# Attention emitted in steps, operands one piece at a time, reciprocals as powers on GpSimd

## Chip, cores and metric

One Trainium2 chip, one core. The metric is the device time of one execution in microseconds, the median of several runs. Engines are called PE (TensorE), DVE (VectorE), ACT (ScalarE), POOL (GpSimd) and SP (SyncE, which issues most DMAs here); PEld is PE's weight load.

## What is computed

Two transformer-like blocks run one after the other over 1024 tokens of width 1024 in fp32. The second one has, between two gated feed-forward layers, a mixer whose first half is attention: eight heads of width 64, three dilated causal windows merged by their softmax denominators. The reference, cut to the attention:

```python
DILATED_BRANCHES = ((128, 1), (512, 4), (2048, 16))

def dilated_window_branch(q, k, v, slopes, window, dilation):
    ...
    s = jnp.einsum('brnqhe,brnkhe->brnhqk', qb, kk) * (HEAD_DIM ** -0.5)
    ...
    s = jnp.where(valid[None, None, :, None], s + bias, -jnp.inf)
    m = jnp.max(s, axis=-1, keepdims=True)
    p = jnp.exp(s - m)
    denom = jnp.sum(p, axis=-1, keepdims=True)
    o = jnp.einsum('brnhqk,brnkhe->brnqhe', p, vv)
    o = o * jnp.swapaxes(1.0 / denom[..., 0], -1, -2)[..., None]
    ...

def second_block(x, ...):
    ...
        q, k, v, u = jnp.split(proj, [ATTN_WIDTH, 2 * ATTN_WIDTH, 3 * ATTN_WIDTH], axis=-1)
        attn = dilated_attention(q, k, v).astype(x.dtype)
        ssm = s5_mixer(u, ...).astype(x.dtype)
        mixed = jnp.concatenate([attn, ssm], axis=-1) @ w_mix_out[l]
    ...
```

The three windows together are one causal softmax over all 1024 keys with a bias that holds slope, mask and the logarithm of how many windows contain a key; the kernel computes it so.

## The kernel before

The whole program is one long sequence of stages; fp32 products are made from pairs of shortened operands, a high part (hi, wh, ph) and what is left (lo, wl, pl), each product being two or three matmuls. A high part is a copy on ACT into a rounded type, a low part a subtraction on POOL or DVE.

The attention stands in the second mixer (mixer2), after the glu of its other half and ahead of the output projection (down, L455). The glu ends in sigmoids on ACT (L1520) and products on DVE (L1521). The stages around it load weights: raw by DMA on SP, wh on ACT (L351), wl on POOL (L352).

Work is done in 16 units, a unit being one half (512 queries) of one of eight heads. For a head, heads_in makes three operands: qq (the query's high half from ACT in 64 partitions, its low part from POOL, L1568, in the other 64), kd (the key's high part, copied by ACT and by a DMA into the other 64 partitions) and kl (the key's low part, POOL L1569, and its DMA). head_v makes vv, the values' two parts. Then softmax does, for each of the unit's four blocks c of 128 queries, with width w = 128 to 512 in the first half and 640 to 1024 in the second:

- logits on PE: kd (L1601) and kl (L1602) against qq into one PSUM bank;
- DVE adds the bias and finds the minimum of the negated logits (L1604) into P;
- ACT takes the exponential in place and its sum into den (L1607);
- DVE makes the reciprocal of den, one column (L1608);
- POOL scales P by it (L1609).

values, for each of 4 or 8 key tiles kt: PE transposes the blocks of P (L1624), ACT copies them as ph (L1626), DVE makes pl (L1627), PE multiplies both by vv into po (L1628, L1629). At the end ACT and DVE add the halves of po into at (L1631, L1632). After all units hilo makes hi (ACT, L1501) and lo (POOL, L1504) of the four at.

The attention loop calls softmax for a unit and then values for the unit three before, each as a whole; heads_in makes two heads at a time and one pair ahead. What an engine then executes is a fixed queue in order: a scheduler, when the program is built, orders each queue by what is emitted and by its own timing estimates, so neighbouring units mix to some degree. Buffers: 32 tiles of 128x1024 shared by operands and probabilities, 8 PSUM banks, two tiles for bias and other large loads (tag xr).

Of the kernel before, what the change touches and what calls it, by code (L numbers as in the profile page):

```python
# [11 lines left out]
F32 = mybir.dt.float32  # L12
F32R = mybir.dt.float32r
# [5 lines left out]
P = 128  # L19
# [228 lines left out]
class Model:  # L248
# [1308 lines left out]
    def heads_in(self, q, k):  # L1557
# [3 lines left out]
        res = []  # L1561
        for a in range(2):
            me, other = slice(64 * a, 64 * a + 64), slice(64 - 64 * a, 128 - 64 * a)
            qq, kd, kl = self.u("qq", F32R), self.u("kd", F32R), self.u("kl", F32R)
            nc.scalar.activation(qq[me], q[me], AF.Copy)
            nc.scalar.activation(kd[me], k[me], AF.Copy)
            nc.sync.dma_start(out=kd.bitcast(F32)[other], in_=kd.bitcast(F32)[me])
            nc.gpsimd.tensor_tensor(qq[other], q[me], qq.bitcast(F32)[me], op=ALU.subtract)  # L1568
            nc.gpsimd.tensor_tensor(kl[me], k[me], kd.bitcast(F32)[me], op=ALU.subtract)  # L1569
            nc.sync.dma_start(out=kl.bitcast(F32)[other], in_=kl.bitcast(F32)[me])  # L1570
            res.append((qq, kd, kl))
        return res
# [9 lines left out]
    def softmax(self, ops, bias, half):  # L1582
# [3 lines left out]
        if half:  # L1586
            ps = [self.u("P") for _ in range(4)]
        else:
            two = [self.u("P", shape=[P, 2, H]) for _ in range(2)]
            ps = [two[c // 2][:, c % 2] for c in range(4)]  # L1590
        mx, den = self.sm("mx", 8), self.sm("den", 4)
        for c, p in enumerate(ps):
# [15 lines left out]
            nc.vector.reciprocal(den[:, c : c + 1], den[:, c : c + 1])  # L1608
            nc.gpsimd.tensor_scalar(out=p[:, :w], in0=p[:, :w], scalar1=den[:, c : c + 1], scalar2=None, op0=ALU.mult)  # L1609
        return ps  # L1610

    def values(self, vv, a, ps, half, at):
# [6 lines left out]
        for kt in range(last + 1):  # L1619
# [9 lines left out]
            nc.tensor.matmul(po[:, sl], vv[:, kt, :], pl[:, sl], start=False, stop=kt == last)  # L1629
        t = self.tmp("vo")  # L1630
        nc.scalar.activation(t[me], po[other], AF.Copy)  # L1631
        nc.vector.tensor_tensor(at[me, half * H : half * H + H], po[me], t[me], op=ALU.add)  # L1632

    def attention(self, qk):

        at, late = [], []
        ops = [self.heads_in(*qk[0])]
        for j in range(4):
            at.append(self.u("at"))
            for a in range(2):  # L1640
                h = 2 * j + a
                bias = self.raw(self.a["bias"][h], name="bias", tag="xr")
                if a == 0 and j < 3:
                    ops.append(self.heads_in(*qk[j + 1]))
                vv = self.head_v(h)
                for half in range(2):
                    ps = self.softmax(ops[j][a], bias, half)
                    late.append((vv, a, ps, half, at[j]))
                    if len(late) > 3:
                        self.values(*late.pop(0))  # L1650
        while late:
            self.values(*late.pop(0))
        return [self.hilo(t) for t in at]
# [71 lines left out]
```

## Time and profile before

| | us |
|---|---|
| median of 3 runs (3076.66 to 3080.45) | 3077.05 |
| the profiled execution | 3082.47 |
| its span | 3080.7 |
| PE busy | 2821.6 (92%) |
| DVE busy | 1775.9 (58%) |
| ACT busy | 1323.5 (43%) |
| POOL busy | 868.0 (28%) |

All trace times are counted from the start of that span. The page cuts the span into 40 slices of 77.0 us and gives each engine's busy share in tenths; the groups of instructions give busy time, mean duration and the idle time ahead of them; the waits say who waited for whom. A share over the whole span says little of one stage, so the rows below are mostly of the attention, 2089.5 to 2271 us.

### The profile page before, as it was taken

Reading aid. Unit: us, or ns where it says so; the run is one execution under the profiler, and the core shown is the slowest. Engines: PE = TensorE matmul, PEld = TensorE weight load, DVE = VectorE, ACT = ScalarE, POOL = GpSimd, SP = SyncE. Lnnn points to the kernel's source line nnn. Section 1 sums busy time; section 2 is a strip of 40 time slices with the busy share of each in tenths; the row PEclk is TensorE's granted clock in tenths of the full one; section 3 lists DMA queues with packets and bytes.
Section 4 is the critical chain, followed back from the end, with each engine's and each line's share of the span. In section 5 each row is a group of like instructions: output and inputs, shape, how many; then the busy total and the mean of one; then the engine's idle time right before and its main releaser. Section 6 shows DMA issues by size and latency. Waiting matters only on the chain.

```text
span 3080.7 us, 33834 instructions
## 1 busy us (share of the span) xinstructions
PE 2821.6 (92%) x12585; PEld 2306.2 (75%) x12585; DVE 1775.9 (58%) x2527; ACT 1323.5 (43%) x1921; POOL 868.0 (28%) x667
## 2 busy tenths in 40 slices
PE   8998999898999979999978999997689899998998
PEld 7777788677777858777767778886677677776776
DVE  4576655487784365665667551417635756665445
ACT  5446555433445463333324452246644533333343
POOL 3331332211222432121111031459844212211002
PEclk9999999999999989999989999998899999999999
DMA  3114344564455123454466661523113244446556
GB/s 141 61 42 137 132 146 146 201 230 144 162 183 170 55 82 103 151 177 150 146 221 212 217 220 72 168 76 110 35 48 130 86 150 158 158 157 208 181 180 209
DMA packets 192309, 443.11 MB, mean 144 GB/s; under 512 B 23220, under 2 KB 23312, under 8 KB 192144
## 3 DMA queue, kind: packets, MB, share of 16 engines
q1 hardware_dynamic: 155600, 362.83, 35.4%
q10 hardware_dynamic: 36544, 78.13, 7.2%
q8 instruction: 98, 1.61, 0.2%
q14 instruction: 67, 0.55, 0.1%
HBM read 303.92 MB, written 131.60 MB: 141 GB/s over the span
## 4 chain that ended last, share of the span: by engine, by line
PE 62%; DMA 14%; DVE 9%; ACT 6%; issue 6%; POOL 2%; SPq 1%; ACTq 0%; DVEq 0%; POOLq 0%
PE b L541 22%; PE b L717 17%; PE b L455 4%; PE b L442 4%; DMA raw<-in_f_out 3%; DMA raw<-in_f_in 3%; DMA td<-tw 2%; DMA tw<-raw 2%; PE b L1103 2%; PE b L1101 2%; PE b L1102 2%; DMA sd<-hs 1%; ACT wh L481 1%; PE b L1624 1%; DVE wl L482 1%
## 5 line engine op out<-in xcount | busy, mean ns | idle before, releaser
L541 PE MATMUL b<-zh,wh 128*128 128x512 f32 x1680 | 644.9, 397 | 30.5 <-ACT wh L481 23.1
L541 PE MATMUL b<-zh,wl 128*128 128x512 f32 x1680 | 623.3, 392 | 8.4 <-DVE wl L482 3.3
L541 PE MATMUL b<-zl,wh 128*128 128x512 f32 x1560 | 612.8, 393 | 15.4 <-DVE zl L211 15.4
L717 PE MATMUL b<-tt,wh 128*128 128x512 f32 x1232 | 392.1, 400 | 51.8 <-ACT tt L698 46.5
L541 PEld LDWEIGHTS b<-zh,wh 128*128 128x128 f32 x1680 | 319.5, 190 | 117.2 <-ACT wh L481 35.1
L541 PEld LDWEIGHTS b<-zh,wl 128*128 128x128 f32 x1680 | 316.8, 189 | 78.6 <-DVE wl L482 4.6
L717 PE MATMUL b<-wl,wh 128*128 128x512 f32 x1344 | 323.5, 402 | 40.3 <-ACT wl L698 26.3
L541 PEld LDWEIGHTS b<-zl,wh 128*128 128x128 f32 x1560 | 295.4, 189 | 79.5 <-DVE zl L211 19.2
L717 PEld LDWEIGHTS b<-wl,wh 128*128 128x128 f32 x1344 | 258.7, 194 | 102.4 <-ACT wl L698 27.8
L717 PEld LDWEIGHTS b<-tt,wh 128*128 128x128 f32 x1232 | 237.5, 194 | 106.8 <-ACT tt L698 48.9
L482 POOL TENSOR_TENSOR wl<-raw,wh 128x1024 fp32r<-128x1024 f32 x60 | 148.0, 2469 | 392.4 <-ACT wh L481 368.9
L698 ACT ACTIVATE wh<-sd 128x1024 fp32r<-128x1024 f32 x140 | 141.7, 1014 | 254.3 <-PE b L717 127.0
L717 PE MATMUL b<-tt,wl 128*128 128x512 f32 x616 | 244.1, 397 | 0.0
L352 POOL TENSOR_TENSOR wl<-raw,wh 128x1024 fp32r<-128x1024 f32 (+1 forms) x58 | 142.6, 2464 | 305.0 <-ACT wh L351 274.1
L481 ACT ACTIVATE wh<-raw 128x1024 fp32r<-128x1024 f32 x120 | 126.8, 1059 | 226.0 <-DMA raw<-in_f_in 102.6
L383 POOL TENSOR_SCALAR v<-ss 128x1 f32<-128x1 f32 x80 | 46.4, 580 | 497.6 <-ACT junk L376 493.9
L618 POOL TENSOR_TENSOR hw<-h 128x512 f32<-128x512 f32 x38 | 59.2, 1558 | 409.2 <-DVE h L1188 173.2
L699 DVE TENSOR_TENSOR tt<-td,tt 128x1024 fp32r<-128x1024 f32 x84 | 95.2, 1134 | 115.4 <-ACT tt L698 115.2
L698 ACT ACTIVATE tt<-td 128x1024 fp32r<-128x1024 f32 x84 | 83.0, 988 | 162.7 <-DMA td<-tw 86.2
L699 DVE TENSOR_TENSOR wl<-sd,wh 128x1024 fp32r<-128x1024 f32 x84 | 97.4, 1159 | 77.1 <-ACT wh L698 77.1
L505 DVE TENSOR_TENSOR s<-raw 128x512 f32<-128x512 f32 x60 | 75.2, 1253 | 115.2 <-DMA raw<-in_f_in 105.2
L717 PEld LDWEIGHTS b<-tt,wl 128*128 128x128 f32 x616 | 119.1, 193 | 25.3
(362 smaller groups left out, 5301.0 us busy)
## 6 DMA issues: line engine op xcount, KB each, us to landing
sd<-hs SPq DMA_DIRECT2D x126, 512.0 KB, 4.0
raw<-in_f_in SPq DMA_DIRECT2D x94, 512.0 KB, 3.5
raw<-in_f_out SPq DMA_DIRECT2D x44, 512.0 KB, 3.6
tw<-raw SPq DMA_DIRECT2D x44, 512.0 KB, 2.9
wd<-in_w_down ACTq DMA_DIRECT2D x40, 512.0 KB, 8.9
td<-tw ACTq DMA_DIRECT2D x40, 512.0 KB, 4.3
hs<-h SPq DMA_DIRECT2D x38, 512.0 KB, 3.3
hs<-hw SPq DMA_DIRECT2D x38, 512.0 KB, 3.1
```

Of the source, the lines that this page charges most:

```text
L352: nc.gpsimd.tensor_tensor(l, r, h.bitcast(F32), op=ALU.subtract)
L442: nc.tensor.matmul(pp[n], w[:, k, :], z(m, k, slice(n * H, n * H + H)), start=k == 0 and w is wh and m == 0, stop=k == nk - 1 and w is wl)
L455: yield nc.tensor.matmul(pp, h[:, ts], w[:, sl], start=f == 0 and w is wh and h is hh, stop=f == len(hs) - 1 and h is hl)
L481: nc.scalar.activation(hi.rearrange("p a b -> p (a b)"), x, AF.Copy)
L482: eng.tensor_tensor(lo.rearrange("p a b -> p (a b)"), x, hi.bitcast(F32).rearrange("p a b -> p (a b)"), op=ALU.subtract)
L505: v.tensor_tensor(s1, a21, a22, op=ALU.add)
L541: self.mark = nc.tensor.matmul(bank, w, x, start=start and k == 0 and i == 0, stop=k == 3 and i == 2, skip_group_check=True)
L698: nc.scalar.activation(hi[:, :n], x[:, :n], AF.Copy)
L699: v.tensor_tensor(lo[:, :n], x[:, :n], hi.bitcast(F32)[:, :n], op=ALU.subtract)
L717: self.mark = nc.tensor.matmul(bank, x[:, c, ts], y[:, c], start=start and k == 0, stop=stop and k == 2, skip_group_check=True)
L1101: nc.tensor.matmul(pp, zh, wh[:, k % 2, :], start=k == 0, stop=False)
L1102: nc.tensor.matmul(pp, zh, wl[:, k % 2, :], start=False, stop=False)
```

## The change

The units and their arithmetic stay, apart from the reciprocal. softmax and values become generators that stop after a query block and after a key tile. attention steps them in turn: for step n, values of unit n-3 (LAG = 3) by key tiles, and between them the query blocks of unit n, so that four blocks are spread over four or eight key tiles. heads_in becomes head_in, which returns two pieces for one head, left (qq) and right (kd, kl); with head_v as third piece, they are emitted one at a time in the second and fourth block of a step, for the next head only. The bias of the next head is requested at the start of a head. The four DVE reciprocals of a unit become one power of -1 on POOL over all four columns of den (128x4, against a tile mone of -1), and the four scalings on POOL follow it.

```diff
-    def heads_in(self, q, k):
...
+    def head_in(self, q, k, a, res):
...
+        def left():
+            qq = self.u("qq", F32R)
             nc.scalar.activation(qq[me], q[me], AF.Copy)
+            nc.gpsimd.tensor_tensor(qq[other], q[me], qq.bitcast(F32)[me], op=ALU.subtract)
+            res.append(qq)
+
+        def right():
+            kd, kl = self.u("kd", F32R), self.u("kl", F32R)
             nc.scalar.activation(kd[me], k[me], AF.Copy)
             nc.sync.dma_start(out=kd.bitcast(F32)[other], in_=kd.bitcast(F32)[me])
-            nc.gpsimd.tensor_tensor(qq[other], q[me], qq.bitcast(F32)[me], op=ALU.subtract)
             nc.gpsimd.tensor_tensor(kl[me], k[me], kd.bitcast(F32)[me], op=ALU.subtract)
             nc.sync.dma_start(out=kl.bitcast(F32)[other], in_=kl.bitcast(F32)[me])
-            res.append((qq, kd, kl))
-        return res
+            res.extend((kd, kl))
+
+        return [left, right]
...
-            nc.vector.reciprocal(den[:, c : c + 1], den[:, c : c + 1])
+            yield
+        nc.gpsimd.tensor_tensor(den, den, self.mone, op=ALU.pow)
+        for c, p in enumerate(ps):
+            w = (4 * half + c + 1) * P
             nc.gpsimd.tensor_scalar(out=p[:, :w], in0=p[:, :w], scalar1=den[:, c : c + 1], scalar2=None, op0=ALU.mult)
-        return ps
...
             nc.tensor.matmul(po[:, sl], vv[:, kt, :], pl[:, sl], start=False, stop=kt == last)
+            if kt < last:
+                yield
...
+    LAG = 3
...
-                if a == 0 and j < 3:
-                    ops.append(self.heads_in(*qk[j + 1]))
-                vv = self.head_v(h)
-                for half in range(2):
-                    ps = self.softmax(ops[j][a], bias, half)
-                    late.append((vv, a, ps, half, at[j]))
-                    if len(late) > 3:
-                        self.values(*late.pop(0))
...
+        def prepare(h):
+
+            ops, vv = [], []
+            bias = self.raw(self.a["bias"][h], name="bias", tag="xr")
+            heads[h] = ops, bias, vv
+            return [*self.head_in(*qk[h // 2], h % 2, ops), lambda: vv.append(self.head_v(h))]
+
+        for f in prepare(0):
+            f()
+        for n in range(16 + self.LAG):
+            h, half = divmod(n, 2)
+            soft = None
+            if h < 8:
...
+                    todo = prepare(h + 1) if h < 7 else []
+                ops, bias, vv = heads[h]
+                ps = []
+                soft = self.softmax(ops, bias, half, ps)
+                late.append((vv[0], h % 2, ps, half, at[h // 2]))
+            val, nk = None, 4
+            if n >= self.LAG:
+                job = late.pop(0)
+                val, nk = self.values(*job), 4 + 4 * job[3]
+            for k in range(nk):
+                if val:
+                    next(val, None)
+                if soft and k * 4 % nk == 0:
+                    next(soft)
+                    if k * 4 // nk in (1, 3) and todo and (half or k * 4 // nk == 1 or len(todo) > 2):
+                        todo.pop(0)()
+            if soft:
+                next(soft, None)
```

The queues of the built program, at three places. POOL around the operands of a head, before: numbers behind a name tell buffers apart, P and den are a unit's probabilities and sums, four query blocks of 128 to 512 being the first half of a head and 640 to 1024 the second.

```order
L1568 TENSOR_TENSOR qq_15533<-qk_14977,qq_15533 64x1024
L1569 TENSOR_TENSOR kl_15535<-qk_14980,kd_15534 64x1024
L1568 TENSOR_TENSOR qq_15542<-qk_14977,qq_15542 64x1024
L1569 TENSOR_TENSOR kl_15544<-qk_14980,kd_15543 64x1024
L1609 TENSOR_SCALAR P_15554<-P_15554,den_15557 128x128
L1609 TENSOR_SCALAR P_15554<-P_15554,den_15557 128x256
L1609 TENSOR_SCALAR P_15555<-P_15555,den_15557 128x384
L1609 TENSOR_SCALAR P_15555<-P_15555,den_15557 128x512
L1609 TENSOR_SCALAR P_15672<-P_15672,den_15677 128x640
L1609 TENSOR_SCALAR P_15673<-P_15673,den_15677 128x768
L1609 TENSOR_SCALAR P_15674<-P_15674,den_15677 128x896
L1609 TENSOR_SCALAR P_15675<-P_15675,den_15677 128x1024
```

The same place in the changed program, operands of one head and one pair of units:

```order
L1566 TENSOR_TENSOR qq_15785<-qk_14977,qq_15785 64x1024
L1615 TENSOR_TENSOR den_15752<-den_15752,mone_15277 128x4
L1573 TENSOR_TENSOR kl_15902<-qk_14980,kd_15901 64x1024
L1615 TENSOR_TENSOR den_15872<-den_15872,mone_15277 128x4
L1618 TENSOR_SCALAR P_15749<-P_15749,den_15752 128x128
L1618 TENSOR_SCALAR P_15749<-P_15749,den_15752 128x256
L1618 TENSOR_SCALAR P_15750<-P_15750,den_15752 128x384
L1618 TENSOR_SCALAR P_15750<-P_15750,den_15752 128x512
L1618 TENSOR_SCALAR P_15867<-P_15867,den_15872 128x640
L1618 TENSOR_SCALAR P_15868<-P_15868,den_15872 128x768
L1618 TENSOR_SCALAR P_15869<-P_15869,den_15872 128x896
L1618 TENSOR_SCALAR P_15870<-P_15870,den_15872 128x1024
```

Before, the operands of two heads come in a row and then scalings alone. Now one head's qq and kl stand between the powers, the power of the second half stands ahead of the first half's scalings, and all eight scalings follow in a row.

POOL at the end of the attention, where lo are the low halves of the finished at; the last of the scalings before:

```order
L1609 TENSOR_SCALAR P_16650<-P_16650,den_16652 128x384
L1609 TENSOR_SCALAR P_16650<-P_16650,den_16652 128x512
L1609 TENSOR_SCALAR P_16767<-P_16767,den_16772 128x640
L1609 TENSOR_SCALAR P_16768<-P_16768,den_16772 128x768
L1609 TENSOR_SCALAR P_16769<-P_16769,den_16772 128x896
L1609 TENSOR_SCALAR P_16770<-P_16770,den_16772 128x1024
L1504 TENSOR_TENSOR lo_17074<-at_15295,hi_17073 128x1024
L1504 TENSOR_TENSOR lo_17078<-at_15530,hi_17077 128x1024
L1504 TENSOR_TENSOR lo_17082<-at_15979,hi_17081 128x1024
```

and now:

```order
L1615 TENSOR_TENSOR den_16624<-den_16624,mone_15277 128x4
L1504 TENSOR_TENSOR lo_17028<-at_15293,hi_17027 128x1024
L1504 TENSOR_TENSOR lo_17032<-at_15516,hi_17031 128x1024
L1615 TENSOR_TENSOR den_16741<-den_16741,mone_15277 128x4
L1504 TENSOR_TENSOR lo_17036<-at_15953,hi_17035 128x1024
L1618 TENSOR_SCALAR P_16621<-P_16621,den_16624 128x128
L1618 TENSOR_SCALAR P_16621<-P_16621,den_16624 128x256
L1618 TENSOR_SCALAR P_16622<-P_16622,den_16624 128x384
L1618 TENSOR_SCALAR P_16622<-P_16622,den_16624 128x512
L1618 TENSOR_SCALAR P_16736<-P_16736,den_16741 128x640
L1618 TENSOR_SCALAR P_16737<-P_16737,den_16741 128x768
L1618 TENSOR_SCALAR P_16738<-P_16738,den_16741 128x896
```

Three of the four low halves moved from behind the last eight scalings to ahead of them, next to the last power.

PE where the logits of a head's first half begin, with P the transposes of an earlier unit; before:

```order
L1601 MATMUL b_15773<-kd_15308,qq_15307 128x128
L1602 MATMUL b_15773<-kl_15309,qq_15307 128x128
L1601 MATMUL b_15780<-kd_15308,qq_15307 128x256
L1602 MATMUL b_15780<-kl_15309,qq_15307 128x256
L1601 MATMUL b_15787<-kd_15308,qq_15307 128x384
L1602 MATMUL b_15787<-kl_15309,qq_15307 128x384
L1629 MATMUL po_15722<-pl_15729,vv_15403 128x512
L1601 MATMUL b_15794<-kd_15308,qq_15307 128x512
L1602 MATMUL b_15794<-kl_15309,qq_15307 128x512
```

The same in the changed program, from the third of the head's kd matmuls (the first two, with eight transposes behind each, stand just ahead of this piece):

```order
L1607 MATMUL b_15810<-kd_15683,qq_15567 128x384
L1636 MATMUL po_15737<-ph_15763,vv_15376 128x512
L1637 MATMUL po_15737<-pl_15764,vv_15376 128x512
L1632 MATMUL b_15815<-idn_78,P_15431 128x128
L1632 MATMUL b_15815<-idn_78,P_15432 128x128
L1632 MATMUL b_15815<-idn_78,P_15433 128x128
L1636 MATMUL po_15737<-ph_15774,vv_15376 128x512
L1637 MATMUL po_15737<-pl_15775,vv_15376 128x512
L1632 MATMUL b_15825<-idn_78,P_15432 128x128
L1632 MATMUL b_15825<-idn_78,P_15433 128x128
L1636 MATMUL po_15737<-ph_15793,vv_15376 128x512
L1608 MATMUL b_15753<-kl_15684,qq_15567 128x128
```

Before, each kd matmul has its kl matmul directly behind it. Now the kd matmuls of three blocks and 21 transposes of the other unit come first and the kl matmuls after them. On SP the order was bias, kd, kd, bias, kl, kl for a pair of heads and is now kd, bias, kl for one head.

## Rows read from the trace of the kernel before

**Rows 1.** page, busy tenths of PE and POOL in 40 slices of the span

```profile
PE   8998999898999979999978999997689899998998
...
POOL 3331332211222432121111031459844212211002
```

**Rows 2.** end of the attention: PE's timeline, then the chain of work

```profile
2259.55 0.30 PE L1624 MATMUL b<-idn,P 128*128 128x128 f32 x1
...
2271.08 19.13 PE b L455 x76
```

**Rows 3.** busy time of each engine by stage; columns in the first line

```profile
core 0: us, PE busy (x) PEld busy (x) DVE busy (x) ACT busy (x) POOL busy (x), PEclk, DMA share, GB/s
2089.50:2271.00 181.50, 130.33 (x674) 109.04 (x673) 125.51 (x378) 125.12 (x267) 145.46 (x80) 0.87 0.18 55
...
2105.90:2205.60 99.70, 69.50 (x358) 60.02 (x358) 66.81 (x212) 68.47 (x148) 98.80 (x54) 0.83 0.20 55
2205.60:2248.60 43.00, 31.45 (x173) 27.05 (x172) 31.12 (x96) 29.45 (x66) 27.35 (x17) 0.90 0.08 26
```

**Rows 4.** waits in the attention: engine, line, releaser, us, times, longest

```profile
PE po L1628 <- ACT ph L1626: 36.7, 17, 7.8
...
POOL P L1609 <- DVE den L1608: 15.6, 5, 6.2
...
PE b L1624 <- POOL P L1609: 6.5, 3, 3.7
```

**Rows 5.** timeline of POOL: start, us, instructions [idle before, releaser]

```profile
2100.66 2.92 POOL L1609 TENSOR_SCALAR P<-P,den 128x128 f32<-128x128 f32 x3
...
2240.99 7.61 POOL L1609 TENSOR_SCALAR P<-P,den 128x768 f32<-128x768 f32 x3 [0.15 <-DVE den L1608]
2248.56 7.07 POOL L1504 TENSOR_TENSOR lo<-at,hi 128x1024 fp32r<-128x1024 f32 x3
```

**Rows 6.** groups of POOL in the attention: busy us, mean ns, idle before

```profile
L1609 POOL TENSOR_SCALAR P<-P,den 128x640 f32<-128x640 f32 (+5 forms) x64 | 109.6, 1734 | 15.9 <-DVE den L1608 15.6
L1568 POOL TENSOR_TENSOR qq<-qk,qq 64x1024 fp32r<-64x1024 f32 x4 | 9.9, 2480 | 0.3
...
L1569 POOL TENSOR_TENSOR kl<-qk,kd 64x1024 fp32r<-64x1024 f32 x4 | 9.5, 2383 | 0.3
```

**Rows 7.** DMA issues: KB each, median us to landing

```profile
kl<-kl SPq DMA_DIRECT2D x8, 256.0 KB, 3.8
```

**Rows 8.** small operations: by line (min/median/max ns), then groups

```profile
L383 POOL TENSOR_SCALAR v<-ss x80: 190/248/1287, 6.2 to 3071.4; 128x1 f32<-128x1 f32 x80
...
L384 POOL TENSOR_TENSOR r<-v,mh x80: 547/548/1617, 6.5 to 3072.2; 128x1 f32<-128x1 f32 x80
...
L1379 POOL TENSOR_TENSOR ph<-s5p,s5k 128x4 f32<-128x4 f32 x8 | 2.0, 253 | 24.2 <-DVE h L1183 20.6 <-DVE sxb L1325 3.6
...
L1608 DVE RECIPROCAL den<-den 128x1 f32<-128x1 f32 x64 | 9.2, 154 | 8.1 <-ACT P L1607 7.9
```

**Rows 9.** timeline of PE and ACT around the first exponentials

```profile
2089.32 0.62 PE L442 MATMUL b<-hi,wl 128*128 128x512 f32 x2
...
2091.22 1.06 ACT L351 ACTIVATE wh<-raw 128x1024 fp32r<-128x1024 f32 x1 [5.65 <-DMA raw<-in_w_mo]
2092.19 1.25 ACT L1520 ACTIVATE gs<-b,cv 128x512 f32<-128x512 f32 x2
...
2093.45 1.28 ACT L1607 ACT_TABLE_LOAD   x1
2094.75 0.40 ACT L1607 ACTIVATE P<-P,mx 128x128 f32<-128x128 f32 x1
...
2098.72 0.71 ACT L1607 ACTIVATE P<-P,mx 128x512 f32<-128x512 f32 x1
...
2115.45 1.04 ACT L1565 ACTIVATE qq<-qk 64x1024 fp32r<-64x1024 f32 x1
```

**Rows 10.** waits of the later stages

```profile
PE b L717 <- ACT tt L698: 10.2, 2, 5.1
```

More of the change, by code (lines that the diff above doesn't have):

```diff
@@ L1555, in v_proj @@
                     self.nc.scalar.activation(o, i, AF.Copy)
[L1557 removed]
+    def head_in(self, q, k, a, res):
         nc = self.nc
[L1561 to L1564, printed above, removed]
+        me, other = slice(64 * a, 64 * a + 64), slice(64 - 64 * a, 128 - 64 * a)
+        def left():
+            qq = self.u("qq", F32R)
             nc.scalar.activation(qq[me], q[me], AF.Copy)
+            nc.gpsimd.tensor_tensor(qq[other], q[me], qq.bitcast(F32)[me], op=ALU.subtract)
+            res.append(qq)
+        def right():
+            kd, kl = self.u("kd", F32R), self.u("kl", F32R)
             nc.scalar.activation(kd[me], k[me], AF.Copy)
             nc.sync.dma_start(out=kd.bitcast(F32)[other], in_=kd.bitcast(F32)[me])
[L1568 removed]
             nc.gpsimd.tensor_tensor(kl[me], k[me], kd.bitcast(F32)[me], op=ALU.subtract)
             nc.sync.dma_start(out=kl.bitcast(F32)[other], in_=kl.bitcast(F32)[me])
[L1571 to L1572 removed]
+            res.extend((kd, kl))
+        return [left, right]
     def head_v(self, h):
@@ L1580, in head_v, with softmax @@
         return vv
-    def softmax(self, ops, bias, half):
+    def softmax(self, ops, bias, half, ps):
         nc = self.nc
@@ L1586, in softmax @@
         if half:
-            ps = [self.u("P") for _ in range(4)]
+            ps.extend(self.u("P") for _ in range(4))
         else:
             two = [self.u("P", shape=[P, 2, H]) for _ in range(2)]
-            ps = [two[c // 2][:, c % 2] for c in range(4)]
+            ps.extend(two[c // 2][:, c % 2] for c in range(4))
         mx, den = self.sm("mx", 8), self.sm("den", 4)
@@ L1632, in values @@
         nc.vector.tensor_tensor(at[me, half * H : half * H + H], po[me], t[me], op=ALU.add)
+    LAG = 3
     def attention(self, qk):
[L1636 to L1642, printed above, removed]
-                if a == 0 and j < 3:
-                    ops.append(self.heads_in(*qk[j + 1]))
-                vv = self.head_v(h)
-                for half in range(2):
-                    ps = self.softmax(ops[j][a], bias, half)
-                    late.append((vv, a, ps, half, at[j]))
-                    if len(late) > 3:
-                        self.values(*late.pop(0))
-        while late:
-            self.values(*late.pop(0))
+        nc = self.nc
+        self.mone = self.sm("mone", 4)
+        nc.vector.memset(self.mone, -1.0)
+        at, late, heads = [], [], {}
+        def prepare(h):
[9 more added lines that the diff above has]
+            if h < 8:
+                if half == 0:
+                    if h % 2 == 0:
+                        at.append(self.u("at"))
+                    todo = prepare(h + 1) if h < 7 else []
[16 more added lines that the diff above has]
+                next(soft, None)
         return [self.hilo(t) for t in at]
```

## The prediction

> **What bounds the kernel now.** I began with the page. PE falls to 7, 6 and 8 tenths in three slices near 2080 to 2310 us, and exactly there POOL, elsewhere mostly at 1 to 4 tenths, reaches 9, 8 and 4 [rows 1]. That is the attention, the only place where the change acts: the first logits follow the glu at 2089.5, and the output projection (L455) starts at 2271.08 [rows 2], 181.5 us in all. The table of stages splits it: over the whole stretch PE is busy 130.3, DVE 125.5, ACT 125.1 and POOL 145.5 us, so POOL is fullest; from 2105.9 to 2205.6 POOL is busy 98.8 of 99.7 us, with PE at 69.5, DVE at 66.8 and ACT at 68.5 [rows 3]. In those 100 us POOL is the bound. Afterwards it is not: of the 43 us from 2205.6 on, it is busy 27.4 [rows 3], and it waits 15.6 us for reciprocals that DVE has not reached [rows 4].
>
> The waits mislead here. The largest by far is PE's for ACT's copy of the transposed probabilities, 36.7 us; PE's direct wait for POOL's scaling is only 6.5 us [rows 4]. But those transposes read probabilities that POOL scaled, and every engine works in order, so a POOL that is behind also holds the logits queued behind the transposes. An edit that removes the 36.7 us by finer interleaving gains only as far as POOL lets it.
>
> POOL's queue: the scaling (L1609) starts at 2100.66, its last three instructions run from 2240.99 to 2248.60, and three low halves of the output (lo, L1504) come after it [rows 5]. From the last scaling to L455 pass another 22.5 us, in which the values of the last units run.
>
> **The change part by part.**
>
> *Values by key tiles between logits.* It adds no arithmetic; it removes phases in which ACT does only exponentials or only copies. As long as POOL is the bound this is worth nothing in the middle. It is worth something at two places, both inside the sum below: POOL's idle 15.9 us (scaling row, [rows 6]) goes, and at the end the values of fewer units are still open.
>
> *Operands one head at a time.* Before, the operands of heads 0 to 3 (eight POOL instructions qq, kl) were made under the glu, where POOL cost nothing, and eight more inside the attention [rows 6]. Now only head 0 and the qq of head 1 come before the first power; kl of head 1 and both of heads 2 to 7, 13 instructions, stand in the POOL-bound queue. At (2.48+2.38)/2 = 2.43 us [rows 6] that is 31.6 us where it was 19.4. DMAs: kd and kl of a head leave SP singly, and the load of the next-but-one bias now stands between them; kl takes 3.8 us to land [rows 7]. On ACT the copies are only spread.
>
> *Reciprocals.* 64 DVE instructions of 154 ns go [rows 8]; DVE is not the bound and the 9.2 us are hidden by POOL, so I count nought. Sixteen POOL powers of 128x4 come, none of which the trace shows. The nearest rows [rows 8]: the same power on 128x1 takes 547 ns in its undisturbed cases, a 128x1 tensor_scalar 190 ns at least, a 128x4 product 253 ns. So one column's power costs about 547-190 = 357 ns over the frame. If one pass serves all four columns, a power is 253+357 = 0.61 us; if columns follow each other, 253+4x357 = 1.68 us. Outer bounds are 0.55 (four columns no dearer than one) and 4x547 = 2.19 us. The rows do not decide between one pass and four; I take the middle, 1.15 us: 16x1.15 = 18.4 us, all on POOL.
>
> *A rule that speaks against this edit.* The rows say that a one-column reciprocal is 154 ns on DVE and a one-column power 547 ns on POOL [rows 8]. The Trainium skill, "GPSIMD Engine Reference", section 4.1 Engine selection, says to put elementwise work on VectorE, GpSimd being about half as fast on two inputs; the trace agrees in direction and is harsher for this operation. By that factor of two a power would be an estimate of 0.3 us, and the sum below would end 13.6 us earlier; I do not use it.
>
> *A wait is added.* The scaling of a unit's first row block no longer starts after its own exponential but after the power of all four, and the queue even puts the power of the head's second unit before the first unit's scaling. Behind that power eight scalings and the next head's operands are queued. The values lag three units, so nobody needs these scalings at once: while POOL is busy throughout, its order only has to keep up. Per head POOL needs 109.6/8 = 13.7 of scaling [rows 6], 2x2.43 and 2x1.15: 20.9 us. ACT, next in line, is busy 125.1/8 = 15.6 us per head [rows 3]. So POOL bounds every head, the last ones too.
>
> *Output low halves.* Three of the four (7.07 us [rows 5]) now stand ahead of the last eight scalings, where before they came behind them and cost nothing: 7.1 us.
>
> *Where it starts.* In before the last sigmoid pair of the glu (1.25 us) waited on ACT behind a weight copy that sat idle 5.65 us for its DMA, and the exponentials began at 2094.75 [rows 9]. In the new order that load goes out earlier on SP. The last glu matmul ends at 2089.9; then the pair 1.25, the qq copy of head 1 1.0, the table 1.28, and four exponentials from 0.40 to 0.71, 2.2 together [rows 9]: first power at 2095.7. If the load is as late as before it is 2100.4, 4.7 later.
>
> *Sum.* 2095.7 + powers 18.4 + scaling 109.6 + operands 31.6 + low halves 7.1 = last scaling done at 2262.4 (before: 2248.6). The values of the last unit need it: from their first transpose to L455 were 2271.08-2259.55 = 11.5 us [rows 2], the same instructions as now. So L455 starts at 2273.9 against 2271.1: **+2.8 us**. Gains and costs nearly cancel: the last scaling 13.8 later, the tail after it 11.0 shorter.
>
> *Elsewhere.* The later stages keep their instructions; in the last one a few ACT copies swap places. From 2842 on PE waits for ACT 10.2 us in two places [rows 10], neither among the swapped ones: nought, with 1 us either way.
>
> The profiled execution is 3082.47 us (span 3080.7), 5.4 above the median of the runs, 3077.05. A shift of 2.8 gives 3085.3 in that execution, and against the median **3079.9 us**.
>
> **The rivals.**
> 1. *The power runs column after column* (1.68 us, up to 2.19). 16x0.53 = 8.5 more: +11.3, 3088; at 2.19, 3096.5. It decides from 1.36 us on, where the loss passes 6.2 us. For it: 357 ns for a single column is long, so a loop of four may well be four times that. Against: part of it may be set-up.
> 2. *The power is one pass* (0.61 us): -5.8, 3071; at 0.55, 3070.
> 3. *The operands arrive late.* A head's kl leaves POOL only after the scaling of the head before last, takes 3.8 us to land [rows 7] behind a bias load that waits for the old bias to be read, and PE has it behind 21 transposes. If the two softmaxes then need over 20.9-3.8 = 17.1 us, POOL idles at the head's second power. 15.6 us of ACT work leaves 1.5 us of margin; if the phases lose 2 us beyond that in six heads: +12, about 3092.
> 4. *The change does what it is for*: POOL's spans are called rough; were POOL not the bound, interleaving could halve PE's 36.7 us wait for ACT: -18, 3059. Against it stand 98.8 of 99.7 us without a gap [rows 3].
>
> **How the numbers follow.** The forecast (power between 0.8 and 1.35, POOL without gaps, +-6) 0.40; rival 1 0.28; rival 2 0.14; rival 3 0.10; rival 4 0.08. 0.2%, about what a measurement of this kernel can tell from no change, is 6.2 us. Faster: rival 4 and a third of rival 2, 0.13. Slower: rival 1 nearly whole 0.27, rival 3 0.10, and 0.04 of the forecast with the late start: 0.41. The rest, 0.46, is the same. The range goes from 3068 (the cheapest power with a start 2 us earlier; most of rival 4 is left out) to 3097 (the dearest power).
>
> **What would show it.** In the new trace POOL should run without gaps from about 2096 until the last eight scalings, ending near 2262, and L455 should start near 2274. The 128x4 power's mean is the first row to read: each 0.1 us is 1.6 us of the end. PE's wait for the kl matmuls, and POOL's idle time before a power, tell rival 3. The forecast is wrong if POOL shows gaps of over 5 us in the middle, if the scaling itself changes its time per element, or if L455 moves and the total does not.

## The result: slower by 0.8%, and the profile after

The changed kernel takes 3102.60 us (median of 4 runs, 3097.24 to 3103.73) against 3077.12 us of the kernel before on the same chip: ratio 1.0082, 95% interval 1.0067 to 1.0097. The forecast was 3079.9 us, its range ended at 3097. The profiled execution took 3102.98 us, its span is 3101.0.

The page of the changed kernel, to be read against [rows 1]: busy tenths and granted clock in 40 slices of 77.5 us.

```profile
PE   9998999889999979999969989996779899998998
...
POOL 3331333211223432121111032358854211211002
PEclk9999999999999989999989999997889999999999
```

The loss is in the same three slices: PE falls to 6, 7 and 7, and POOL no longer reaches 9 there. To compare kernels, I measure the attention from the start of the glu's last two matmuls (L442) to the first L455, since the glu ends anywhere between 2077 and 2092 us from one profile to the next. Before that was 2089.32 to 2271.08 [rows 9, 2], 181.8 us, and the forecast put it at 2273.9-2089.3 = 184.6. Now it is 2086.74 to 2294.14: **207.4 us, 25.6 more**. The two medians differ by 25.5 us. The two profiled executions differ by 20.5 only, since the rest of the span is 5.3 us shorter in the second; that is no more than the spread of the changed kernel's four runs (6.5 us).

Busy time by stretch of the changed kernel (columns as in [rows 3]): the attention, then the three parts of the forecast's sum, up to the first power, from there to the end of the last scaling, and the tail.

```profile
2086.74:2294.14 207.40, 143.84 (x675) 120.70 (x673) 122.16 (x313) 130.69 (x271) 170.49 (x99) 0.79 0.17 49
2086.74:2094.03 7.29, 4.93 (x27) 4.15 (x25) 6.47 (x13) 6.96 (x14) 5.10 (x3) 1.00 0.63 217
2094.03:2281.30 187.27, 130.37 (x609) 109.91 (x609) 110.45 (x292) 117.05 (x246) 164.47 (x96) 0.78 0.16 46
2281.30:2294.14 12.84, 8.55 (x39) 6.64 (x39) 5.24 (x9) 6.68 (x12) 0.91 (x1) 0.77 0.00 0
```

The parts were forecast as 6.4, 166.7 and 11.5 us; they are 7.3, 187.3 and 12.8. So 20.6 of the 22.8 us of error lie in the middle, which the forecast took to be filled by POOL. POOL is busy 164.5 of these 187.3 us. Its groups there (busy us, mean ns | idle before), beside [rows 6]:

```profile
L1618 POOL TENSOR_SCALAR P<-P,den 128x128 f32<-128x128 f32 (+3 forms) x64 | 109.7, 1736 | 0.2
L1573 POOL TENSOR_TENSOR kl<-qk,kd 64x1024 fp32r<-64x1024 f32 x7 | 17.4, 2484 | 0.5 <-ACT kd L1571 0.2
L1566 POOL TENSOR_TENSOR qq<-qk,qq 64x1024 fp32r<-64x1024 f32 x7 | 17.0, 2424 | 0.6
L1615 POOL TENSOR_TENSOR den<-den,mone 128x4 f32<-128x4 f32 x16 | 16.4, 1024 | 17.8 <-ACT P L1613 17.4
```

POOL's work is what was forecast, the powers a little cheaper (1.02 us for 1.15). New are 17.8 us of idle time ahead of the powers. The waits in the attention, beside [rows 4] (us, times, longest):

```profile
PE po L1636 <- ACT ph L1634: 42.6, 19, 6.1
...
ACT ph L1634 <- PE b L1632: 41.5, 28, 4.3
...
POOL den L1615 <- ACT P L1613: 17.4, 6, 5.0
...
ACT P L1613 <- DVE mx L1610: 15.5, 16, 3.0
```

PE's wait for ph, 36.7 us before, is not removed but has grown. One of the five gaps of 1.9 to 5.0 us ahead of a power, in POOL's timeline:

```profile
2160.43 2.40 POOL L1573 TENSOR_TENSOR kl<-qk,kd 64x1024 fp32r<-64x1024 f32 x1 [0.19 <-ACT kd L1571]
2167.87 1.01 POOL L1615 TENSOR_TENSOR den<-den,mone 128x4 f32<-128x4 f32 x1 [5.04 <-ACT P L1613]
2168.87 13.65 POOL L1618 TENSOR_SCALAR P<-P,den 128x128 f32<-128x128 f32 x8
```

The power of a head's second half waits for its fourth exponential, with eight scalings behind it. This power starts at 2119.40, 2142.02, 2167.87, 2191.27, 2216.15, 2239.54 and 2264.33: a head takes 24.2 us on average, not 20.9. Why the exponential is late is seen in ACT, DVE and PE around that gap:

```profile
2163.33 0.59 ACT L1641 ACTIVATE vo<-po 64x512 f32<-64x512 f32 x1
2163.83 0.62 ACT L1583 ACTIVATE vv<-v 128x512 fp32r<-128x512 f32 x1
2166.55 1.15 ACT L1613 ACTIVATE P<-P,mx 128x1024 f32<-128x1024 f32 x1 [2.11 <-DVE mx L1610]
2167.61 0.19 ACT L1613 ACTIVATION_READ_ACCUMULATOR P<-P,mx 128x1 f32 x1
2167.82 0.60 ACT L1634 ACTIVATE ph<-b 128x512 fp32r<-128x512 f32 x1
...
2163.96 0.68 DVE L1642 TENSOR_TENSOR at<-po,vo 64x512 f32<-64x512 f32 x1 [1.62 <-ACT vo L1641]
2164.56 0.67 DVE L1610 CUSTOM_DVE_ANT_0 P<-b,bias 128x512 f32<-128x512 f32 x1
2165.17 0.68 DVE L1584 TENSOR_TENSOR vv<-v,vv 128x512 fp32r<-128x512 f32 x1
2165.77 0.74 DVE L1610 CUSTOM_DVE_ANT_0 P<-b,bias,mx 128x512 f32<-128x512 f32 x1
...
2162.64 0.41 PE L1632 MATMUL b<-idn,P 128*128 128x128 f32 x2
2168.47 0.79 PE L1636 MATMUL po<-ph,vv 128*128 128x512 f32 x1 [5.42 <-ACT ph L1634]
```

At the end of the step everything goes in single file. ACT's vo releases DVE's sum at; behind it stand both bias additions of the widest block with vv between; ACT, whose next instruction is that block's exponential, waits 2.11 us for them; and the first ph copy of the next step, whose transposes PE finished long ago, stands behind that exponential. PE can do nothing without the copy and sits idle 5.42 us. The logits behind that matmul, their bias additions and their exponentials are late with it, and POOL meets them a head later; this last link is read from the order of the queues, not measured.

The first change of heads also costs something: PE waits there 6.3 us for kd and 2.5 for kl. ACT copies kd only at 2093.91, behind the first four exponentials; its DMA leaves at once, at 2094.99, and lands 2.8 us later. The DMA of kl leaves at 2098.16, behind the load of a bias. This happens once, and the 6.3 us stand in every kernel below that has single operands. Groups of PE, whole attention:

```profile
L1607 PE MATMUL b<-kd,qq 128*128 128x384 f32 (+2 forms) x96 | 40.3, 428 | 6.3 <-DMA kd<-kd 6.3
...
L1608 PE MATMUL b<-kl,qq 128*128 128x384 f32 (+2 forms) x96 | 34.3, 385 | 2.5 <-DMA kl<-kl 2.5
```

### The profile page after: what moved, and what is told of

Read it like the earlier page. It is cut to its first block, busy times and chain, and to the rows that moved or that the text cites. A ratio compares the mean times of both kernels' runs of the same rounds, so it can differ in the third digit from the quotient of the medians.

```text
span 3101.0 us, 33817 instructions
## 1 busy us (share of the span) xinstructions
PE 2836.6 (91%) x12585; PEld 2318.5 (75%) x12585; DVE 1771.4 (57%) x2464; ACT 1325.4 (43%) x1921; POOL 881.3 (28%) x683
## 5 line engine op out<-in xcount | busy, mean ns | idle before, releaser
L541 PEld LDWEIGHTS b<-zl,wh 128*128 128x128 f32 x1560 | 295.5, 189 | 76.3 <-DVE zl L211 16.4
L383 POOL TENSOR_SCALAR v<-ss 128x1 f32<-128x1 f32 x80 | 46.9, 587 | 492.1 <-ACT junk L376 484.2
```

The lines of the kernel that those rows point to most:

```text
L383: nc.gpsimd.tensor_scalar(out=v, in0=ss, scalar1=1.0 / D, scalar2=EPS, op0=ALU.mult, op1=ALU.add)
L541: self.mark = nc.tensor.matmul(bank, w, x, start=start and k == 0 and i == 0, stop=k == 3 and i == 2, skip_group_check=True)
```

## Experiments

The table gives the attention from L442 to L455 in one profile each, PE's wait for ph there (in all, and the longest), and the time as a ratio to the kernel before on the same chip. Letters: S steps, O operands one piece at a time, P powers.

| kernel | attention us | PE for ph, us | ratio [95% interval] |
|---|---|---|---|
| before | 181.8 | 36.7 (7.8) | 1 |
| S (e5) | 181.4 | 29.7 (3.6) | 0.9999 [0.9986, 1.0012] |
| O (e6) | 186.3 | 26.8 (3.7) | 1.0002 [0.9987, 1.0018] |
| P (e4) | 185.5 | 31.0 (3.9) | 1.0009 [0.9998, 1.0020] |
| S O (e1) | 183.1 | 28.3 (2.5) | 1.0015 [1.0005, 1.0025] |
| O P (e3) | 185.8 | 22.7 (3.1) | 1.0019 [1.0009, 1.0029] |
| S P (e2) | 198.1 | 29.2 (4.2) | 1.0061 [1.0046, 1.0076] |
| S O P (changed) | 207.4 | 42.6 (6.1) | 1.0082 [1.0067, 1.0097] |
| changed, power behind scalings (e9) | 204.8 | 35.6 (6.4) | 1.0065 [1.0041, 1.0090] |
| changed, one DVE reciprocal a unit (e10) | 187.0 | 30.5 (6.0) | 1.0016 [1.0004, 1.0028] |
| changed, ph ahead (e13) | 189.0 | 20.6 (3.4) | 1.0044 [1.0027, 1.0061] |
| S O, exponential ahead (e14) | 198.2 | 46.9 (6.8) | 1.0053 [1.0032, 1.0074] |
| S O, ph ahead (e20) | 187.6 | 29.0 (2.8) | 1.0020 [1.0004, 1.0035] |
| S P, ph ahead (e19) | 197.9 | 26.0 (3.5) | 1.0047 [1.0032, 1.0061] |
| S O, sums scaled (e11) | 167.8 | 25.0 (2.2) | 0.9964 [0.9951, 0.9977] |
| before, sums scaled (e12) | 162.9 | 24.3 (2.4) | 0.9941 [0.9921, 0.9960] |
| e12, values one unit behind (e15) | 167.8 | 28.1 (3.3) | 0.9970 [0.9957, 0.9984] |

The two measures agree to about 7 us (0.2%): 25.6 us of 3077 are 0.83%, 16.3 are 0.53%. Two kernels that differ by less are not told apart here. The ratio is taken from all runs on a chip and can differ a little from that of two medians.

**Which part?** Three theories came first: A, the operands arrive late, since the bias load stands ahead of kl on SP; B, the steps make the engines wait for one another; C, the powers. Each part was undone in the changed kernel: the powers (e1), the single operands (e2), the steps (e3); and powers alone were put into the kernel before (e4).

e1, against the changed kernel:

```diff
+            nc.vector.reciprocal(den[:, c : c + 1], den[:, c : c + 1])
+            nc.gpsimd.tensor_scalar(out=p[:, :w], in0=p[:, :w], scalar1=den[:, c : c + 1], scalar2=None, op0=ALU.mult)
             yield
-        nc.gpsimd.tensor_tensor(den, den, self.mone, op=ALU.pow)
-        for c, p in enumerate(ps):
...
```

e2, against the changed kernel (pair(j) makes the operands of two heads at once):

```diff
-                    todo = prepare(h + 1) if h < 7 else []
-                ops, bias, vv = heads[h]
+                    bias = self.raw(self.a["bias"][h], name="bias", tag="xr")
+                    if h % 2 == 0 and h < 6:
+                        ops2.append(pair(h // 2 + 1))
+                    vv = [self.head_v(h)]
+                ops = ops2[h // 2][h % 2]
```

e3, against the changed kernel (softmax of a unit whole, then values of a unit whole):

```diff
-            for k in range(nk):
-                if val:
-                    next(val, None)
...
+            if n >= self.LAG:
+                for _ in self.values(*late.pop(0)):
+                    pass
```

e4, against the kernel before:

```diff
-            nc.vector.reciprocal(den[:, c : c + 1], den[:, c : c + 1])
...
+        nc.gpsimd.tensor_tensor(den, den, self.mone, op=ALU.pow)
+        for c, p in enumerate(ps):
...
```

> The changed kernel (3102.6) with the reciprocals back on DVE, one per block of 128 queries, each followed at once by its scaling on POOL; steps and single operands stay. Theory A (a head's operands arrive late, behind the bias load on SP, and POOL idles before a head's second power): at most 5 us of the 25 come back, about 3098. Theory B (the steps lock the queues together at each step's end: last copies, last logits, last exponential, first copy of the next step): about 3095, since a scaling no longer waits for all four exponentials but the lock stays. Theory C (the sixteen powers and their wait are the cost): nearly all comes back, about 3080.

> The changed kernel with operands as before: both heads of a pair in a row, one pair ahead, bias and values operand at the head's own start; steps and powers stay. A: 3080 to 3085, POOL's idle time before powers falls from 17.4 us to under 5. B: about 3098, the idle time stays. C: about 3100.

> The changed kernel without steps: a unit's softmax is emitted whole and then the values of the unit three before, whole, as in the kernel before; single operands and powers stay. A: about 3100. B: about 3083. C: about 3098.

> The kernel before (3077) with the powers alone: sixteen POOL powers of 128x4 in place of 64 DVE reciprocals, the four scalings of a unit behind the power. POOL gets 16 x 1.02 = 16.4 us more, of which its 15.6 us of idle time at the end can hide some. A and B: 3080 to 3088. C: 3095 or more.

A falls as the main cause: with operands in pairs 9.3 of the 25.6 us come back in the profile, but the loss is still 0.6%. B and C fall as single causes too: without powers, or without steps, most comes back, and powers alone cost 0.1%. It takes steps and powers together. e3 is of note for the forecast's sum: without steps POOL idles only 1.4 us ahead of its powers, and 4.0 us of the loss remain.

**The order of POOL's queue?** In the changed kernel the second half's power stands ahead of the first half's four scalings (4.27 us), which could fill the gap. Theory Q blames that order, G the powers' 16.4 us, L the waits among PE, ACT and DVE. e9 puts each power behind the scalings of the unit before; e10 replaces the power by one DVE reciprocal over four columns; e11 and e12 take the scaling off POOL altogether.

e9, against the changed kernel (after sets an order in a queue and adds no wait):

```diff
-        nc.gpsimd.tensor_tensor(den, den, self.mone, op=ALU.pow)
+        power = nc.gpsimd.tensor_tensor(den, den, self.mone, op=ALU.pow)
+        if self.scaled:
+            self.after(power, self.scaled)
...
```

e10, against the changed kernel:

```diff
-        nc.gpsimd.tensor_tensor(den, den, self.mone, op=ALU.pow)
+        nc.vector.reciprocal(den, den)
```

e11 against e1 and e12 against the kernel before (the reciprocals are kept as ps[4] and spread over the partitions as rb):

```diff
-            nc.gpsimd.tensor_scalar(out=p[:, :w], in0=p[:, :w], scalar1=den[:, c : c + 1], scalar2=None, op0=ALU.mult)
...
+        rb = self.bank("rb")
+        for c in range(4):
+            nc.tensor.transpose(rb[:, c * P : (c + 1) * P], ps[4][:, c : c + 1].to_broadcast([P, P]), self.idn)
...
-        nc.vector.tensor_tensor(at[me, half * H : half * H + H], po[me], t[me], op=ALU.add)
+        nc.vector.tensor_tensor(t[me], po[me], t[me], op=ALU.add)
+        nc.vector.tensor_tensor(at[me, half * H : half * H + H], rb[me], t[me], op=ALU.mult)
```

> The changed kernel, with one rule more for the order of GpSimd's queue: a unit's power stands behind the last scaling of the unit before. All work stays. Theory Q (queue order: in the changed kernel the power of a head's second half, which waits for its fourth exponential, stands ahead of the first half's four scalings, 4.27 us, that could run meanwhile): POOL's idle time ahead of the powers falls from 17.4 us to under 6, the first L455 after the attention starts at 2272 to 2281 (changed kernel 2294.1), ratio to before 1.001 to 1.004. Theory G (GpSimd's added 16.4 us of powers is the cost, whatever the order): 2290 or later, ratio 1.006 to 1.008. Theory L (PE, ACT and DVE wait for one another at the end of each step, and GpSimd only shows it): idle stays at 14 or more, 2290 or later, ratio 1.006 to 1.008.

> The changed kernel with the power replaced by one DVE reciprocal over the four columns of den, still behind the unit's fourth exponential. GpSimd keeps only scalings and operands. Theory G (the powers' 16.4 us): first L455 at 2268 to 2278, ratio 1.000 to 1.002. Theory Q (a blocked queue): gives back as well, if the first half's scalings come to stand ahead of the wait: 2268 to 2278. Theory L, or a batch of four that costs by itself since no scaling can start before the fourth exponential: 2285 or later, ratio 1.005 or more.

> Steps and single operands of the changed kernel, DVE reciprocals column by column, and no scaling of P on GpSimd at all (110 us less of its work): the unit's sum of values is scaled once instead, by the reciprocals that PE spreads over the partitions with four transposes of a repeated column (4 x 0.24 us a unit), one more DVE product of 64x512 a unit (0.69 us, 11 us in all). If GpSimd bounds the attention in all these kernels (theories Q and G): the first L455 10 to 25 us ahead of the 2267.3 of steps with operands and DVE reciprocals, ratio to before 0.992 to 0.997. If the lockstep of PE, ACT and DVE bounds it (theory L): 2262 to 2270, ratio 0.999 to 1.003.

> The kernel before with the same replacement: no scaling of P on GpSimd, the sums of values scaled once (PE 4 x 0.24 us and DVE 0.69 us more a unit). GpSimd as the bound: the first L455 10 to 25 us ahead of the 2271.1 of before, ratio 0.992 to 0.997. PE, ACT and DVE as the bound: within 4 us of 2271.1, ratio 0.999 to 1.002.

Q falls: e9's idle ahead of the powers is gone (1.9 us with that of the scalings), yet the attention is only 2.6 us shorter. The idle time moved to the operands, in POOL's waits of e9:

```profile
POOL qq L1566 <- ACT qq L1565: 9.6, 2, 6.2
```

So POOL waits for ACT wherever its queue places the wait. e10 keeps the wait for all four exponentials and gains 20.4 us, so that wait alone is not the cost either. G still fitted both. L had expected 2285 or later for e10, whose first L455 comes at 2275.68; but e10 also has another order on ACT, as the next part shows. e11 and e12 show that POOL's scaling is what limits the kernel before, as the prediction read: without it the attention is 18.9 us shorter (e12), and 15.2 shorter in the stepped kernel (e11 against e1). Both also take a link out of the chain from exponential to transposes, so they do not tell POOL's time from that link. Busy times of e12's attention, beside the 145.7 us of POOL before:

```profile
2088.48:2251.34 162.86, 127.80 (x739) 104.85 (x737) 135.58 (x394) 124.36 (x267) 36.57 (x16) 0.96 0.21 62
```

**The order at the end of a step?** ACT's queue differs between S O, e10 and changed above all at two places. The first ph copy of the next step stands ahead of the widest exponential (1024) in about every second head with DVE reciprocals, in no head of the changed kernel or of e9. And with DVE reciprocals the exponentials of a first half stand behind the last copies of a step, not among them, in about every second head. Theory H says that the first of these is the loss. e13 forces the copy ahead in the changed kernel, keeping all its work and leaving the second difference as it is; e14 does the converse where there are no powers; e5 is the steps alone.

e13, against the changed kernel (the first e is the exponential, the second the ph copy):

```diff
+            if c == 3 and half:
+                self.last_exp = e
...
+            if kt == 0 and half and self.last_exp:
+                self.after(self.last_exp, e)
+                self.last_exp = None
```

e14 has the same lines in e1, but for one:

```diff
-                self.after(self.last_exp, e)
+                self.after(e, self.last_exp)
```

e5 is the kernel before with the loop of steps, operands in pairs and reciprocals as before.

> The changed kernel, all its work and its powers kept, with one rule for the order of ACT's queue: the exponential of a head's widest block (1024) stands behind the first ph copy of the next step's values. In the changed kernel it stands ahead of it in every head, in the kernels with reciprocals on DVE behind it in about every second. Theory H (order at the end of a step: that copy waits behind an exponential that DVE isn't ready for, and PE, with its queue in order, waits for the copy): PE's 5 us waits at the ends of steps go, POOL's idle time ahead of the powers falls from 17.4 to under 10, the first L455 comes 10 to 18 us earlier than the changed kernel's 2294.1, ratio to before 1.001 to 1.004. Theory G (GpSimd's added 16.4 us): no earlier than 2290, ratio 1.006 or more.

> The converse: steps, single operands and DVE reciprocals column by column (first L455 at 2267.3, ratio 1.0015), with the widest exponential always ahead of the first ph copy of the next step's values. No power is in it. Theory H: the loss comes without any power, first L455 at 2277 or later, ratio 1.004 to 1.008. Theory G: 2264 to 2271, ratio 1.000 to 1.003.

> The kernel before with the steps alone: operands in pairs, DVE reciprocals column by column. Theory H: what the order at the ends of steps makes of it, 2267 to 2290. Theory G: without powers nothing lost, 2264 to 2273, ratio 0.999 to 1.002.

e13's first L455 is at 2268.30, but its glu ended 7.4 us earlier than in the changed kernel; from L442 on the gain is 18.4 us, the upper end of what H expected; the ratio, 1.0044, is just above its 1.004. By the ratios the gain is smaller, 0.38% or some 12 us, with intervals that do not meet (1.0067 and more before, 1.0061 and less now). G, which had expected no gain, falls. POOL's groups and the waits of e13:

```profile
L1620 POOL TENSOR_SCALAR P<-P,den 128x128 f32<-128x128 f32 (+3 forms) x64 | 110.0, 1737 | 1.2
...
L1617 POOL TENSOR_TENSOR den<-den,mone 128x4 f32<-128x4 f32 x16 | 17.2, 1077 | 0.7 <-ACT P L1613 0.7
```

```profile
PE po L1641 <- ACT ph L1636: 20.6, 19, 3.4
...
PE b L1634 <- POOL P L1620: 12.7, 10, 2.5
```

The idle time ahead of the powers fell from 17.8 to 0.7 us and PE's wait for ph halved; its wait for P that POOL scales grew from 5.1 to 12.7. POOL now runs as forecast; its second-half scalings start 20.9 us apart:

```profile
2119.93 9.40 POOL L1620 TENSOR_SCALAR P<-P,den 128x640 f32<-128x640 f32 x4
...
2140.90 9.41 POOL L1620 TENSOR_SCALAR P<-P,den 128x640 f32<-128x640 f32 x4
...
2161.62 9.41 POOL L1620 TENSOR_SCALAR P<-P,den 128x640 f32<-128x640 f32 x4
...
2182.40 9.40 POOL L1620 TENSOR_SCALAR P<-P,den 128x640 f32<-128x640 f32 x4
...
2203.39 9.41 POOL L1620 TENSOR_SCALAR P<-P,den 128x640 f32<-128x640 f32 x4
```

And in e13 the end of the step that was shown above, ACT then PE:

```profile
2148.62 0.59 ACT L1646 ACTIVATE vo<-po 64x512 f32<-64x512 f32 x1
2149.12 0.62 ACT L1583 ACTIVATE vv<-v 128x512 fp32r<-128x512 f32 x1
2150.79 0.60 ACT L1636 ACTIVATE ph<-b 128x512 fp32r<-128x512 f32 x1 [1.05 <-PE b L1634]
2151.86 1.15 ACT L1613 ACTIVATE P<-P,mx 128x1024 f32<-128x1024 f32 x1 [0.47 <-DVE mx L1610]
...
2150.37 0.33 PE L1634 MATMUL b<-idn,P 128*128 128x128 f32 x1 [2.21 <-POOL P L1620]
2151.44 0.50 PE L1641 MATMUL po<-ph,vv 128*128 128x512 f32 x1 [0.75 <-ACT ph L1636]
```

The copy now stands ahead of the exponential. PE waits 0.75 us for it where it waited 5.42, and 2.21 us for POOL's scaling ahead of the last transpose: here POOL is what PE waits for.

The converse holds as well. e14 has no power at all, and with the exponential ahead of the copy it loses 15.2 us against e1, by the ratios 0.38% again (1.0015 to 1.0053); PE's wait for ph is back:

```profile
PE po L1639 <- ACT ph L1634: 46.9, 19, 6.8
```

Either rule let the scheduler reorder the other queues too, so neither of these pairs isolates the copy. In e13 a first half's scalings now stand ahead of the second half's power, PE's order changed in many places, and in two heads DVE's last bias addition of the widest block moved ahead of vv; in e14 the order of all engines differs from e1's. A cleaner pair is on record: e9 and e13. By names and shapes their DVE and POOL queues in the attention are the same, PE's differ in the place of one transpose, and ACT's only in that the widest exponential goes behind the first copy, in seven heads. From e9 to e13 the attention is 15.8 us shorter (204.8 to 189.0), and PE's wait for ph falls from 35.6 to 20.6. The reordering that both share is worth the 2.6 us of e9. The ratios (1.0065 and 1.0044) point the same way, but their intervals meet.

**What is left of the powers, and the pairs.** e20 puts e13's rule into e1, e19 into e2; e6 is the missing corner, single operands alone.

> Steps and single operands with DVE reciprocals column by column (183.05 us, ratio 1.0015), with the same rule. Against the changed kernel with the rule (189.0 us, ratio 1.0044) it differs in the reciprocals alone. If GpSimd's time bounds once the order is right, it is shorter by what 14 to 16 powers of 1.02 us take: 173 to 177 us, ratio 0.997 to 0.999. If GpSimd doesn't bound without the powers: 181 to 185 us, ratio 0.999 to 1.002.

> Steps and powers with operands in pairs (198.1 us from glu's last matmul to the first L455, ratio 1.0061), with the rule that the widest exponential stands behind the first ph copy of the next step's values. Theory H (the order at the end of a step): 182 to 190 us, ratio 1.000 to 1.003. If the loss there has another cause (the pairs of operands, 9.9 us at a time in GpSimd's queue): 194 or more, ratio 1.005 or more.

> The kernel before with single operands, one piece at a time, alone (no steps, DVE reciprocals). Every theory so far: no loss by itself, 179 to 184 us (before 181.8), ratio 0.999 to 1.001. If late operands were a cause of the loss: 186 or more.

By its edit e20 differs from e13 in the reciprocals alone, and it is 1.4 us shorter in the profile (ratios 1.0020 and 1.0044, with intervals that meet): with the order right, 16.4 us of powers cost little. POOL idles in e20 instead, 13.6 us ahead of qq and 5.5 ahead of its scalings; that PE, ACT and DVE need about as long for a head without the powers as POOL does with them is the likely reason, not a shown one. Neither stretch expected for e20 came, and its ratio is the upper end of the second. Against e1 the rule costs 4.5 us in the profile and nothing clear in the ratio (1.0020 for 1.0015), so a copy ahead of the exponential is not better in every kernel: in e1's three heads where the exponential stands ahead, ACT does not wait for it. e19 speaks against H for that kernel: the rule gives back 0.2 us in the profile, and the ratios (1.0061 and 1.0047) do not tell the two apart. With pairs PE's wait for ph is ordinary, but it waits for the scaled P. The waits of e19, then of e2:

```profile
PE b L1634 <- POOL P L1620: 20.2, 12, 3.9
```

```profile
PE b L1632 <- POOL P L1618: 18.9, 11, 5.4
```

With 9.8 us of operands in one piece in POOL's queue (four of 2.4 to 2.7), scalings come too late for the transposes. That this is the whole of their 16 us is argued, not shown; e2's POOL also idles 13.0 us in two waits for an exponential, after its last operands. e6's profile is 4.6 us longer than before, which is where late operands were expected, at a granted clock of 0.77; its time is not longer (1.0002).

**A kernel that beats both.** e12, the kernel before with the sums of values scaled in place of P, takes 3065.72 us against 3080.28 (medians; ratio from all runs 0.9941). Shortening the distance between softmax and values does not add to it.

e15, against e12:

```diff
-                    if len(late) > 3:
+                    if len(late) > 1:
```

> The kernel before without scaling on GpSimd (sums of values scaled once; ratio 0.994, first L455 at 2251.3), and values one unit behind softmax in place of three. There 28.6 us pass between the last exponential of 1024 and the first L455, since three units of values are left. If P is ready without GpSimd's scaling, the nearer distance mixes these values with logits: first L455 at 2243 to 2250, ratio 0.991 to 0.994. If values then wait for exponentials in their own queues: 2253 or later, ratio 0.995 or more.

e15 did not gain: 167.8 us in place of 162.9, ratio 0.9970, the second of the two outcomes. (Its first L455, at 2244.60, is early only because its glu ended 11.7 us earlier than e12's.) Its PE waits more for ph (28.1 us for 24.3), which fits a distance between softmax and values that hides ACT's copies; no run isolates that.

## Why the prediction was wrong

- **What bounds the kernel** was right for the kernel before, and only just: without POOL's scaling the attention is 18.9 us shorter (e12), but e20, with 16.5 us less work on POOL than e13, is 1.4 us shorter, so the other engines are close behind. PE's large wait for ph was indeed not to be had by finer steps: S alone gives 0.4 us. Rival 4 (-18) is out.
- **Powers:** 1.02 us for the 1.15 taken, 16.4 for 18.4. Neither one pass (0.61) nor column after column (1.68): (1024-547)/3 = 159 ns for each further column. Rivals 1 and 2 are out. By the factor of two that the Trainium skill ("GPSIMD Engine Reference", section 4.1 Engine selection) gives for elementwise add, multiply and max on two inputs, a power was an estimate of 0.3 us; the trace gives 1.02, so the factor does not hold for this operation; DVE's reciprocal of the same 128x4 takes 175 ns in e10.
- **Scaling, operands, low halves, start:** 109.7 for 109.6 us; operands 2.42 and 2.48 for 2.43; three low halves ahead of the last scalings, 7.0 for 7.1; first power 7.3 us after the start of the glu's last two matmuls for 6.4. The tail took 12.8 for 11.5.
- **The step that failed** is "15.6 us per head. So POOL bounds every head, the last ones too", with "nobody needs these scalings at once: while POOL is busy throughout, its order only has to keep up". Busy time of ACT is not the time that a head takes on it. With an in-order queue on every engine, the end of a step was a chain ACT, DVE, ACT, PE. That order, not POOL's work, made a head take 24.2 us: e13 keeps the work and its heads take 20.9. POOL idled 17.8 us ahead of its powers and 4.5 ahead of the low halves. With the copy ahead (e13), the sum holds in the profile: 167.6 us from the first power (2086.63) to the end of the last scaling (2254.23) against 166.7 forecast. What stays of e13's 4.4 us over 184.6 is 0.9 there, 0.9 at the start and 2.6 in the tail.
- **Rival 3** named the symptom, POOL idle before the second power of a head, with a chance of 0.10 and 12 us above the forecast. The cause it gave, a late kl, is not it: PE waits for kd and kl at one change of heads only, 8.8 us, and with operands in pairs, where these waits are gone, 16.3 us of loss stay. A late exponential for a reason of order in ACT's queue was in no rival.
- **Open:** why the scheduler puts the exponential first as soon as the powers are there; no run shows its estimates. e13's time (1.0044, 13.5 us over the kernel before) is some 6 us above what its profile lets expect, so of the 25 us the order is worth 12 by the times and 18 by the profiles, and no run settles that. Why steps and powers lose 16.3 us with operands in pairs, where the rule does not help, is open as well.

## What to carry over

When several engines share a stage, adding up the fullest one's work is a lower bound; before trusting it, walk through one period of the queues and look where an instruction that is needed by an idle engine stands behind one that is not ready. A change of a cheap operation to another engine can reorder queues it never touches, so compare the order of the engines that wait, not only of the engine that gets the work. Where one engine does bound a stage, taking its work away can gain more than any order around it. Here one product of 64x512 a unit and four small transposes, in place of four products of up to 128x1024, gave 18.9 us; the steps gave 0.4.

## What was not expected of the hardware

A GpSimd power costs 547 ns for 128x1 and 1024 ns for 128x4, so on average 159 ns for each further column. TensorE's granted clock, a mean of its two levels of 1.2 and 2.4 GHz, was over the attention 0.79 in the changed kernel, 0.86 in e13 and 0.96 in e12. It does not follow the waits for ph alone: in e6, where they are 26.8 us, it was 0.77. The 675 matmuls of the changed kernel and of e13 are the same, yet PE is busy 143.8 and 136.5 us with them, 7.3 us more at the lower clock; how much of the 18.4 us between the two kernels that makes is not shown. The row of e13's attention, beside that of the changed kernel above:

```profile
2079.33:2268.30 188.97, 136.53 (x675) 111.98 (x673) 119.09 (x313) 129.81 (x271) 171.13 (x99) 0.86 0.18 53
```
